# A gate matrix for 16384 experts: low parts of the weights on VectorE, one-hot rows of two keys in one operation

## The chip, the core and the metric

One core of a Trainium2 chip runs the whole program once. The metric is the time of one launch in device microseconds. Of the kernel before there are three timed runs, with a median of 3199.23 us (3198.02 to 3207.88).

The engines are called TensorE (PE in the profile, its weight loads PEld), VectorE (DVE), ScalarE (ACT), GpSimd (POOL) and SyncE (SP, which issues the DMAs here).

## What is computed

The reference is two transformer blocks, one after the other, on 512 tokens of width 1024, in 32-bit floats. The change touches one layer of the first block, a lookup among 16384 experts, cut to this:

```python
def peer(n, w_q, sub_keys, expert_u, expert_v):      # n: 512 tokens x 1024
    q = (nf @ w_q).reshape(t, PEER_HEADS, D_KEY)
    ...
    v1, i1 = lax.top_k(s1, TOPK)                     # 8 heads, 128 keys on either side
    v2, i2 = lax.top_k(s2, TOPK)
    cand = (v1[..., :, None] + v2[..., None, :]).reshape(t, PEER_HEADS, TOPK * TOPK)
    vals, ci = lax.top_k(cand, TOPK)
    ...
    idx = (e1 * N_KEYS + e2).reshape(t, PEER_HEADS * TOPK)
    gates = jax.nn.softmax(vals.astype(jnp.float32), axis=-1)
    ...
        ug = expert_u[ib]
        act = jax.nn.gelu(jnp.einsum("td,tkd->tk", xb, ug)) * gb
        vg = expert_v[ib]
        return jnp.einsum("tk,tkd->td", act, vg)
```

So each token has 128 chosen experts (8 heads times 16), named by a pair of keys (e1, e2) of 128 each, and a gate for each of them.

## The kernel before

The kernel does not gather experts. It treats all 16384 as a dense layer: hidden = gelu(expert_u x tokens), multiplied by a gate matrix that is zero where a token did not choose the expert, then expert_v x hidden. Hidden units are worked through in 128 rows of 128, one row for each value of the second key; the code calls such a row an expert row, and the texts here say "expert" for it. `up` (line 611) makes one: eight blocks of 128 input columns, each with three matmuls of 128x128 by 128x512 in `mm3` (lines 233 to 235). Three, because a 32-bit weight and a 32-bit input are each split into a high part, rounded to the matmul's format, and a low part, the remainder: high x high, high x low, low x high.

The weights come through `Stream` (line 77). A tile holds 16 blocks, so two experts. `fetch` asks SP for the 1 MB transfer into `raw` (three buffers). `block` calls `load_split` (line 210): for either half of 1024 columns ScalarE copies the high part into `wh` (line 216), then GpSimd subtracts it from the raw weight into `wl` (line 217). Both have two buffers (pool `sp`): one tile in use, one being made.

The layer has these steps. `route` makes queries, scores and the top 16 on VectorE (`top16`, line 799), and 37 experts run on TensorE beside it (`IN_ROUTE`). Then `build_g` (line 810) makes the gate matrix and the generator `fill`, which is `spills` over `up`, gives it the other 35 of the first 72 experts (`SPILL`). Their activations go to memory in groups of four (`act_d`). Then the main part goes over all 32 groups of experts: the gate is multiplied in (`gated`) and `down` adds the result to the tokens; the modulation vector of the second block (`ada`) is made beside it.

In `build_g` the partitions hold the 128 choices of a token. A pass of the loop handles `TB` = 8 tokens, so there are 64 passes. `hots` makes the one-hot rows with four VectorE operations of 128x1024 in 16 bits: `o1` (line 837) compares the first key with 0 to 127, `o2` (line 838) the second, and `og` (line 842), twice, multiplies `o2` by the high and by the low part of the gate. To keep runs of four adjacent values, keys and gates are first repeated four times (`repeated`, line 824; `DUP` = 4). TensorE multiplies `o1` by `og` (line 861), 16 matmuls a pass (two a token), ScalarE copies the sums from two PSUM buffers to `gs` (line 865), and every fourth pass SP writes 2 MB of it to `g_d` (line 869). `o1` has two buffers, `o2` one, `og` four, which is two passes of its two parts.

The order of the work: the program text gives priorities, and the framework lays out each engine's queue ahead of time from them, from the operands' dependences and from when buffers come free, so that an instruction can stand in its queue ahead of others that are earlier in the text. Only instructions named in `keep_in_program_order` are pinned. On the chip each queue is run strictly in order. One pass of the text is:

```python
            if t0 + TB < S:
                nxt = hots(t0 + TB)
            left = SPILL - IN_ROUTE
            if t0 // TB * left % (S // TB) < left:
                next(fill, None)
```

so one-hots are made a pass ahead, and an expert is run in 35 of the 64 passes, spread evenly: never do two passes in a row go without one.

Of the kernel before, what the change touches and what calls it, by code (L numbers as in the profile page):

```python
# [10 lines left out]
F32 = mybir.dt.float32  # L11
F32R = mybir.dt.float32r
BF16 = mybir.dt.bfloat16
F16 = mybir.dt.float16
# [8 lines left out]
P = 128  # L23
# [53 lines left out]
class Stream:  # L77
    def __init__(self, net, name, ub=UB, chunk=8, loads=1):
        self.net, self.ap, self.w, self.chunk, self.loads = net, net.A[name], ub * P, chunk * P, loads
        self.ub, self.raw, self.have = ub, {}, {}  # L80

    def fetch(self, b):
        if b not in self.raw and b not in self.have:
# [2 lines left out]
    def block(self, b):  # L86
        if b not in self.have:
            self.fetch(b)
            self.have = {k: v for k, v in self.have.items() if k >= b - 1}
            self.have[b] = self.net.load_split(self.raw.pop(b), self.w, self.chunk)  # L90
        return self.have[b]

    def unit(self, u, n=1):
# [31 lines left out]
def run(gen):  # L125
    for _ in gen:
        pass
# [12 lines left out]
class Net:  # L140
# [66 lines left out]
        if self.keeps:  # L207
            self.tc.keep_in_program_order(ins)

    def load_split(self, raw, w, chunk):  # L210
        nc = self.nc
        h = self.sp.tile([P, UB * P], F32R, tag="wh", name=self.nm("wh"))
        lo = self.sp.tile([P, UB * P], F32R, tag="wl", name=self.nm("wl"))
        for o in range(0, w, chunk):
            c = slice(o, min(o + chunk, w))
            self.keep(nc.scalar.copy(h[:, c], raw[:, c]))  # L216
            nc.gpsimd.tensor_tensor(lo[:, c], raw[:, c], h[:, c].bitcast(F32), ALU.subtract)  # L217
        return h, lo

    def split(self, src, tag=None, bufs=1, tags=None):  # L220
# [378 lines left out]
    def peer(self, X, pre=None):  # L599
        nc, tc = self.nc, self.tc  # L600
        act_d = self.dp.tile([SPILL // GE, P, GE, S], F32, tag="act_d", name="act_d")
        g_d = self.dp.tile([S // GB, P, E2, GB], F32, tag="g_d", name="g_d")
        v3 = lambda a: a.rearrange("p (b t) -> p b t", t=GB)
        with self.phase("pk"), ExitStack() as stack:
            ak = stack.enter_context(tc.tile_pool(name="ak", bufs=1, side="right"))
            a4_ = lambda: ak.tile([P, GE, S], F32, tag="a4", name=self.nm("a4"), bufs=2)
            pre = (pre or self.peer_norm(X)).ready()
            ns = pre.hs
            us, vs = Stream(self, "expert_u"), Stream(self, "expert_v")

            def up(gr, a4):
                for j in range(GE):
                    p = self.proj(us, (gr * GE + j) * KD, ns)
                    nc.scalar.activation(a4[:, j, :], p, AF.Gelu_apprx_tanh)
                    yield

            def spills():
                for gr in range(SPILL // GE):
                    a4 = a4_()
                    yield from up(gr, a4)  # L620
                    nc.sync.dma_start(act_d[gr], a4)

            def gated(a4, g4, As, pv):

                for j in range(GE):
                    a = a4[:, j, :]
                    nc.vector.tensor_tensor(v3(a), v3(a), g4[:, :, j, :], ALU.mult)  # L627
                    h, lo = (pv.tile([P, S], F32R, tag=t, name=self.nm(t), bufs=2 * GE) for t in ("ah", "al"))
                    nc.scalar.copy(h, a)  # L629
                    nc.vector.tensor_tensor(lo, a, h.bitcast(F32), ALU.subtract)  # L630
                    As.append((h, lo))
                    yield

            def down(at, As, beside):

                for n in range(KD):
                    p = self.ps()
                    for j in range(GE):
                        self.mm3(p, vs.unit((at * KD + n) * GE + j), As[j], j == 0, j == GE - 1)
                    nc.vector.tensor_tensor(X[n], X[n], p, ALU.add)  # L640
                    next(beside, None)
                run(beside)

            fill = spills()
            with tc.tile_pool(name="pr", bufs=1) as pr:
                e1T, e2T, gT = self.route(pre, pr, fill)
            with tc.tile_pool(name="pb", bufs=1) as pb:
                self.build_g(pb, e1T, e2T, gT, g_d, fill)
            run(fill)
            with tc.tile_pool(name="ad", bufs=1, side="right") as ad, tc.tile_pool(name="pv", bufs=1) as pv:  # L650
                def fetch(at):

                    if at == len(ORDER):
                        return None
                    gr, a4 = ORDER[at], a4_()
                    if gr * GE < SPILL:
                        nc.sync.dma_start(a4, act_d[gr])
                    g4 = ad.tile([P, S // GB, GE, GB], F32, tag="g4", name=self.nm("g4"), bufs=2)
                    nc.sync.dma_start(g4, g_d[:, :, gr * GE : (gr + 1) * GE, :].rearrange("b p e t -> p b e t"))
                    return a4, g4  # L660

                before = None
                mods = self.ada(ad)
                next(mods)
                nxt = fetch(0)
                for at, gr in enumerate(ORDER):
                    (a4, g4), As = nxt, []
                    if gr * GE >= SPILL:
                        for _ in up(gr, a4):
                            next(mods, None)  # L670
                    nxt = fetch(at + 1)
                    parts = gated(a4, g4, As, pv)
                    if gr * GE >= SPILL:
                        parts = chain(parts, (next(mods, None) for _ in range(KD - GE - 1)))
                    if before is None:
                        run(parts)
                    else:
                        down(*before, parts)
                    before = (at, As)
                run(mods)  # L680
                down(*before, iter(()))
# [117 lines left out]

    def top16(self, v, i, s, n):  # L800
        nc = self.nc
        tmp = self.small(n, tag="tk")
        nc.vector.max(v[:, 0:8], s)
        nc.vector.max_index(i[:, 0:8], v[:, 0:8], s)
        nc.vector.match_replace(tmp, v[:, 0:8], s, NEG)
        nc.vector.max(v[:, 8:16], tmp)
        nc.vector.max_index(i[:, 8:16], v[:, 8:16], tmp)

    def build_g(self, pb, e1T, e2T, gT, g_d, fill):
# [1 line left out]

        nc = self.nc
        io = pb.tile([P, P], F16, tag="io", name="io")
        ii = pb.tile([P, P], I32, tag="ioi", name="ioi")
        nc.gpsimd.iota(ii, [[1, P]], channel_multiplier=0)
        nc.vector.tensor_copy(io, ii)
        gh, gl = self.g(F16, "gh"), self.g(F16, "gl")
# [1 line left out]
        nc.vector.tensor_copy(gh, gT)  # L819
        nc.vector.tensor_tensor(gl, gT, gh, ALU.subtract)  # L820

        def repeated(src, tag):
            d = pb.tile([P, S, DUP], F16, tag=tag, name=tag)
            nc.vector.tensor_copy(d, src[:, :, None].to_broadcast([P, S, DUP]))
            return d

        k1, k2 = repeated(e1T, "k1"), repeated(e2T, "k2")
        parts = repeated(gh, "kh"), repeated(gl, "kl")
        four = [P, TB, P // DUP, DUP]
        v4 = lambda a: a.rearrange("p t (k d) -> p t k d", d=DUP)  # L830
        io4 = io.rearrange("p (k d) -> p k d", d=DUP)[:, None, :, :].to_broadcast(four)
        bc = lambda a, t0: a[:, t0 : t0 + TB, None, :].to_broadcast(four)

        def hots(t0):
            oh = lambda tag, bufs: pb.tile([P, TB, P], F16, tag=tag, name=self.nm(tag), bufs=bufs)
            o1, o2 = oh("o1", 2), oh("o2", 1)
            nc.vector.tensor_tensor(v4(o1), io4, bc(k1, t0), ALU.is_equal)
            nc.vector.tensor_tensor(v4(o2), io4, bc(k2, t0), ALU.is_equal)
            og = []
            for part in parts:  # L840
                og.append(oh("og", 4))
                nc.vector.tensor_tensor(v4(og[-1]), v4(o2), bc(part, t0), ALU.mult)
            return o1, og

        gs = None
        nxt = hots(0)
        for t0 in range(0, S, TB):
            o1, og = nxt
            if t0 + TB < S:
                nxt = hots(t0 + TB)  # L850
            left = SPILL - IN_ROUTE
# [4 lines left out]
            for q in range(TB // 4):  # L856
                p = self.ps("gg", 2)
                for i in range(4):
                    t = 4 * q + i
                    for j in range(2):  # L860
                        nc.tensor.matmul(
                            p[:, i * P : (i + 1) * P], o1[:, t, :], og[j][:, t, :], start=(j == 0), stop=(j == 1)
                        )
                r = t0 % GB + 4 * q
                nc.scalar.activation(
                    gs[:, :, r : r + 4], p.rearrange("p (t e) -> p e t", t=4), AF.Copy, scale=1.0 / GSCALE
                )
# [821 lines left out]
```

## Time and profile before

| | us |
|---|---|
| median of three runs | 3199.23 |
| the profiled execution | 3196.37 |
| its span in the trace | 3194.6 |
| TensorE busy in the span | 3048.8 |
| VectorE busy | 1905.5 |
| GpSimd busy | 1465.6 |
| ScalarE busy | 1049.6 |

The profiled execution's own time is 1.8 us more than its span. Busy time of TensorE is modelled, since matmuls are pipelined: a matmul's end in the trace lies behind the start of the next. Its rate is better read from the starts of neighbouring matmuls, or from how many there are in a stretch. A line number is the line of the kernel that issued an instruction; `xN` is how many there are in a row or group; a bracket gives the idle time of the engine just before, and what ended it.

### The profile page before, as it was taken

To read this page: it belongs to the slowest core of one execution; us is meant where nothing else is said; L and a number is where in the kernel's file an instruction comes from. 1 tells how busy PE (TensorE), PEld (TensorE's weight loads), DVE (VectorE), ACT (ScalarE), POOL (GpSimd) and SP (SyncE) were. 2 spreads that over 40 slices of the span, in tenths; PEclk is the share of its full clock that TensorE was granted. 3 is DMA by queue.
4 is the path that set the end of the run, shared out by engine and by line. 5 is a ranking of instruction groups with operands and counts; after the bars stand their busy time and mean duration, and the time that the engine had idled before them with its cause. 6 is when DMAs were issued, how large, how long until landed. Compare 5 with 4: busy or idle time off the path is not lost.

```text
span 3194.6 us, 38906 instructions
## 1 busy us (share of the span) xinstructions
PE 3048.8 (95%) x15428; PEld 2545.1 (80%) x15428; DVE 1905.5 (60%) x3262; ACT 1049.6 (33%) x1632; POOL 1465.6 (46%) x777
## 2 busy tenths in 40 slices
PE   8589999999999999999999988899999999999998
PEld 7478888777878888888888877778888887888887
DVE  8964778988667676676555566666211277552123
ACT  4232222444422322222222344343322234432222
POOL 5635666333345444454444443533444431234454
PEclk9889999999999999999999989999999999999999
DMA  3222333565775656665555311112222221122321
GB/s 135 73 79 93 119 119 139 198 237 208 264 247 197 211 199 207 214 224 193 202 188 177 109 67 60 53 41 79 89 91 105 99 76 38 53 92 76 116 88 65
DMA packets 131926, 424.88 MB, mean 133 GB/s; under 512 B 7824, under 2 KB 73872, under 8 KB 97184
## 3 DMA queue, kind: packets, MB, share of 16 engines
q1 hardware_dynamic: 131744, 422.40, 37.5%
q8 instruction: 121, 1.98, 0.3%
q14 instruction: 61, 0.50, 0.1%
HBM read 367.84 MB, written 54.53 MB: 132 GB/s over the span
## 4 chain that ended last, share of the span: by engine, by line
PE 47%; DVE 5%; issue 1%; ACT 1%; POOL 1%; DVEq 0%; POOLq 0%; ACTq 0%
PE mm L233 15%; PE mm L234 15%; PE mm L235 15%; DVE l L380 1%; PE sm L1239 1%; PE sm L1203 1%; DVE sq L297 0%; DVE m L371 0%; PE gg L1266 0%; PE sm L307 0%; PE gg L1260 0%; DVE x L980 0%; PE mm L1395 0%; PE sm L337 0%; POOL wl L217 0%
## 5 line engine op out<-in xcount | busy, mean ns | idle before, releaser
L217 POOL TENSOR_TENSOR wl<-raw,wh 128x1024 fp32r<-128x1024 f32 (+4 forms) x526 | 1280.2, 2456 | 1544.5 <-ACT wh L216 1537.2
L233 PE MATMUL mm<-h,wh 128*128 128x512 f32 (+1 forms) x2524 | 962.0, 382 | 24.3 <-DVE x L980 7.5
L235 PE MATMUL mm<-h,wl 128*128 128x512 f32 (+1 forms) x2524 | 951.6, 378 | 23.0 <-POOL wl L217 22.9
L234 PE MATMUL mm<-l,wh 128*128 128x512 f32 (+1 forms) x2428 | 924.9, 381 | 16.8 <-DVE l L228 12.4
L216 ACT CAST wh<-raw 128x1024 fp32r<-128x1024 f32 (+4 forms) x526 | 510.1, 996 | 938.1 <-issue 524.1
L235 PEld LDWEIGHTS mm<-h,wl 128*128 128x128 f32 x2524 | 482.0, 191 | 112.7 <-POOL wl L217 26.7
L233 PEld LDWEIGHTS mm<-h,wh 128*128 128x128 f32 x2524 | 482.5, 191 | 111.5 <-DVE x L980 8.7
L234 PEld LDWEIGHTS mm<-l,wh 128*128 128x128 f32 x2428 | 464.6, 191 | 100.6 <-DVE l L228 13.0
L233 PE MATMUL mm<-ah,wh 128*128 128x512 f32 x1024 | 399.3, 390 | 5.3 <-DVE x L640 5.3
L234 PE MATMUL mm<-al,wh 128*128 128x512 f32 x1024 | 399.1, 390 | 0.0
L235 PE MATMUL mm<-ah,wl 128*128 128x512 f32 x1024 | 399.0, 390 | 0.0
L942 DVE CUSTOM_DVE_ANT_0 aw<-aw,c 128x1024 f32<-128x1024 f32 x96 | 199.6, 2081 | 118.0 <-DMA aw<-in_ada_w 94.8
L640 DVE TENSOR_TENSOR x<-x,mm 128x512 f32<-128x512 f32 x256 | 172.6, 681 | 144.5 <-PE mm L235 144.5
L233 PEld LDWEIGHTS mm<-ah,wh 128*128 128x128 f32 x1024 | 192.6, 188 | 46.8 <-DVE x L640 4.4
L234 PEld LDWEIGHTS mm<-al,wh 128*128 128x128 f32 x1024 | 192.5, 188 | 40.1
L235 PEld LDWEIGHTS mm<-ah,wl 128*128 128x128 f32 x1024 | 192.6, 188 | 40.0
L1488 DVE TENSOR_TENSOR sg<-sg,mm 128x512 f32<-128x512 f32 (+1 forms) x48 | 30.9, 643 | 301.4 <-PE mm L235 288.0
L629 ACT CAST ah<-a 128x512 fp32r<-128x512 f32 x128 | 79.4, 621 | 333.8 <-DVE a L627 202.2
L980 DVE SCALAR_TENSOR_TENSOR x<-mm,mod,x 128x256 f32<-128x256 f32 (+1 forms) x112 | 66.5, 595 | 188.5 <-PE mm L235 188.4
L627 DVE TENSOR_TENSOR a<-a,g 128x512 f32<-128x512 f32 x128 | 139.8, 1118 | 61.6 <-DMA a<-act_d 47.4
L630 DVE TENSOR_TENSOR al<-a,ah 128x512 fp32r<-128x512 f32 x128 | 141.2, 1109 | 40.7 <-ACT ah L629 39.5
L233 PE MATMUL mm<-g,wh 128*128 128x512 f32 (+1 forms) x416 | 148.6, 357 | 0.0
(391 smaller groups left out, 3789.4 us busy)
## 6 DMA issues: line engine op xcount, KB each, us to landing
raw<-in_expert_u SPq DMA_DIRECT2D x64, 1024.0 KB, 5.3
raw<-in_expert_v SPq DMA_DIRECT2D x64, 1024.0 KB, 5.1
aw<-in_ada_w SPq DMA_DIRECT2D x96, 512.0 KB, 4.6
raw<-in_ffn_w_in SPq DMA_DIRECT2D x44, 1024.0 KB, 4.8
g_d<-gs SPq DMA_DIRECT2D x16, 2048.0 KB, 7.9
g<-g_d SPq DMA_DIRECT2D x32, 1024.0 KB, 6.3
act_d<-a SPq DMA_DIRECT2D x18, 1024.0 KB, 3.9
a<-act_d SPq DMA_DIRECT2D x18, 1024.0 KB, 4.8
```

What stands on the lines that cost most here:

```text
L216: self.keep(nc.scalar.copy(h[:, c], raw[:, c]))
L217: nc.gpsimd.tensor_tensor(lo[:, c], raw[:, c], h[:, c].bitcast(F32), ALU.subtract)
L233: nc.tensor.matmul(out, w[0], x[0], start=start, stop=False)
L234: nc.tensor.matmul(out, w[0], x[1], start=False, stop=False)
L235: nc.tensor.matmul(out, w[1], x[0], start=False, stop=stop)
L380: nc.vector.scalar_tensor_tensor(lo[:, c], t, sh(k), h[:, c].bitcast(F32), ALU.add, ALU.subtract)
L627: nc.vector.tensor_tensor(v3(a), v3(a), g4[:, :, j, :], ALU.mult)
L629: nc.scalar.copy(h, a)
L630: nc.vector.tensor_tensor(lo, a, h.bitcast(F32), ALU.subtract)
L640: nc.vector.tensor_tensor(X[n], X[n], p, ALU.add)
L942: nc.vector.tensor_tensor_reduce(w, w, c, 1.0, 0.0, ALU.mult, ALU.add, self.mod[:, i : i + 1])
L980: self.nc.vector.scalar_tensor_tensor(x, p, self.mod[:, o + n : o + n + 1], x, ALU.mult, ALU.add)
```

## The change

- `load_split` gets the engine of the subtraction as an argument, GpSimd as before, except for the tiles of `expert_u` that are asked for while `build_g` runs: there it is VectorE.
- In that time `up` asks for the tile of the next expert right behind an expert's activation. For the first expert of a tile this is the same tile, for the second the next one.
- The two keys lie side by side in one tensor, as do the gate's two parts, so that one VectorE operation of 128x2048 makes the one-hots of both keys (`oh`, in place of `o1` and `o2`). The two multiplications stay two, and write the two halves of one `og`. Both tiles have two buffers.
- The scratch of `top16` has two buffers in place of four, and the index tile `ii` comes from the common pool of 512-column tiles.

```diff
     def __init__(self, net, name, ub=UB, chunk=8, loads=1):
...
+        self.eng = net.nc.gpsimd
...
-            self.have[b] = self.net.load_split(self.raw.pop(b), self.w, self.chunk)
+            self.have[b] = self.net.load_split(self.raw.pop(b), self.w, self.chunk, self.eng)
...
-    def load_split(self, raw, w, chunk):
+    def load_split(self, raw, w, chunk, eng):
...
-            nc.gpsimd.tensor_tensor(lo[:, c], raw[:, c], h[:, c].bitcast(F32), ALU.subtract)
+            eng.tensor_tensor(lo[:, c], raw[:, c], h[:, c].bitcast(F32), ALU.subtract)
...
                     nc.scalar.activation(a4[:, j, :], p, AF.Gelu_apprx_tanh)
+                    if us.eng is nc.vector:
+                        us.block((gr * GE + j + 1) * KD // UB)
                     yield
...
+                us.eng = nc.vector
                 self.build_g(pb, e1T, e2T, gT, g_d, fill)
+            us.eng = nc.gpsimd
             run(fill)
...
-        tmp = self.small(n, tag="tk")
+        tmp = self.small(n, tag="tk", bufs=2)
...
-        ii = pb.tile([P, P], I32, tag="ioi", name="ioi")
+        ii = self.g(I32, "ioi")[:, :P]
...
-        def repeated(src, tag):
-            d = pb.tile([P, S, DUP], F16, tag=tag, name=tag)
-            nc.vector.tensor_copy(d, src[:, :, None].to_broadcast([P, S, DUP]))
+        def repeated(two, tag):
+
+            d = pb.tile([P, S, 2, DUP], F16, tag=tag, name=tag)
+            for i, src in enumerate(two):
+                nc.vector.tensor_copy(d[:, :, i, :], src[:, :, None].to_broadcast([P, S, DUP]))
             return d
 
-        k1, k2 = repeated(e1T, "k1"), repeated(e2T, "k2")
-        parts = repeated(gh, "kh"), repeated(gl, "kl")
-        four = [P, TB, P // DUP, DUP]
-        v4 = lambda a: a.rearrange("p t (k d) -> p t k d", d=DUP)
+        keys, gates = repeated((e1T, e2T), "kk"), repeated((gh, gl), "kg")
+        four = [P, 2 * TB, P // DUP, DUP]
+        v4 = lambda a: a.rearrange("p t i (k d) -> p (t i) k d", d=DUP)
         io4 = io.rearrange("p (k d) -> p k d", d=DUP)[:, None, :, :].to_broadcast(four)
-        bc = lambda a, t0: a[:, t0 : t0 + TB, None, :].to_broadcast(four)
+        bc = lambda a, t0: a[:, t0 : t0 + TB].rearrange("p t i d -> p (t i) d")[:, :, None, :].to_broadcast(four)
 
         def hots(t0):
-            oh = lambda tag, bufs: pb.tile([P, TB, P], F16, tag=tag, name=self.nm(tag), bufs=bufs)
-            o1, o2 = oh("o1", 2), oh("o2", 1)
-            nc.vector.tensor_tensor(v4(o1), io4, bc(k1, t0), ALU.is_equal)
-            nc.vector.tensor_tensor(v4(o2), io4, bc(k2, t0), ALU.is_equal)
-            og = []
-            for part in parts:
-                og.append(oh("og", 4))
-                nc.vector.tensor_tensor(v4(og[-1]), v4(o2), bc(part, t0), ALU.mult)
-            return o1, og
+            oh, og = (pb.tile([P, TB, 2, P], F16, tag=t, name=self.nm(t), bufs=2) for t in ("oh", "og"))
+            nc.vector.tensor_tensor(v4(oh), io4, bc(keys, t0), ALU.is_equal)
+            for i in range(2):
+                nc.vector.tensor_tensor(
+                    og[:, :, i, :].rearrange("p t (k d) -> p t k d", d=DUP),
+                    oh[:, :, 1, :].rearrange("p t (k d) -> p t k d", d=DUP),
+                    gates[:, t0 : t0 + TB, i, None, :].to_broadcast([P, TB, P // DUP, DUP]), ALU.mult,
+                )
+            return oh, og
...
-                            p[:, i * P : (i + 1) * P], o1[:, t, :], og[j][:, t, :], start=(j == 0), stop=(j == 1)
+                            p[:, i * P : (i + 1) * P], oh[:, t, 0, :], og[:, t, j, :], start=(j == 0), stop=(j == 1)
```

## Rows read from the trace of the kernel before

**Rows 1.** Windows: start:end, length, then busy us (count) of each engine, clock, DMA.
```profile
core 0: us, PE busy (x) PEld busy (x) DVE busy (x) ACT busy (x) POOL busy (x), PEclk, DMA share, GB/s
...
559.00:829.00 270.00, 257.72 (x1844) 207.69 (x1843) 236.86 (x256) 117.39 (x199) 99.30 (x35) 0.99 0.56 215
...
829.00:860.00 31.00, 31.00 (x139) 25.64 (x138) 12.38 (x14) 13.06 (x17) 13.55 (x6) 1.00 0.90 300
...
1000.00:1100.00 100.00, 100.00 (x443) 82.81 (x442) 72.22 (x69) 30.09 (x40) 51.68 (x20) 1.00 0.56 196
```
**Rows 2.** Timeline of PE, two places: start us, us, engine, line, operation [idle before, releaser].
```profile
609.53 1.07 PE L861 MATMUL gg<-og,o 128*128 128x128 f16 x16
610.40 0.47 PE L233 MATMUL mm<-h,wh 128*128 128x512 f32 x1
610.72 0.39 PE L234 MATMUL mm<-l,wh 128*128 128x512 f32 x1
...
664.28 0.47 PE L233 MATMUL mm<-h,wh 128*128 128x512 f32 x1
665.08 0.23 PE L861 MATMUL gg<-og,o 128*128 128x128 f16 x1 [0.33 <-DVE og L842]
665.68 1.00 PE L861 MATMUL gg<-og,o 128*128 128x128 f16 x15 [0.37 <-DVE og L842]
```
**Rows 3.** Waits in 559 to 829 us: total, times, longest.
```profile
PE gg L861 <- DVE og L842: 11.5, 25, 2.9
```
**Rows 4.** Groups by line in 559 to 829 us: busy us, mean ns, idle before.
```profile
L217 POOL TENSOR_TENSOR wl<-raw,wh 128x1024 fp32r<-128x1024 f32 x35 | 100.4, 2888 | 177.3 <-ACT wh L216 177.3
L837 DVE TENSOR_TENSOR o<-io,k 128x1024 f16<-128x1024 f16 x64 | 78.9, 1232 | 1.6 <-PE gg L861 1.6
L842 DVE TENSOR_TENSOR og<-o,kl 128x1024 f16<-128x1024 f16 x64 | 76.6, 1197 | 0.0
...
L838 DVE TENSOR_TENSOR o<-io,k 128x1024 f16<-128x1024 f16 x64 | 48.4, 756 | 1.7
L842 DVE TENSOR_TENSOR og<-o,kh 128x1024 f16<-128x1024 f16 x64 | 46.2, 721 | 23.9 <-PE gg L861 21.7
```
**Rows 5.** Timelines of POOL and of DVE around one tile's subtractions.
```profile
610.66 5.65 POOL L217 TENSOR_TENSOR wl<-raw,wh 128x1024 fp32r<-128x1024 f32 x2 [8.44 <-ACT wh L216]
...
611.19 2.88 DVE L837 TENSOR_TENSOR o<-io,k 128x1024 f16<-128x1024 f16 x1
613.99 2.87 DVE L842 TENSOR_TENSOR og<-o,kl 128x1024 f16<-128x1024 f16 x1
616.90 0.69 DVE L838 TENSOR_TENSOR o<-io,k 128x1024 f16<-128x1024 f16 x1
617.51 0.68 DVE L837 TENSOR_TENSOR o<-io,k 128x1024 f16<-128x1024 f16 x1
```
**Rows 6.** Timeline of PE at the loop's second pass.
```profile
564.07 0.39 PE L234 MATMUL mm<-l,wh 128*128 128x512 f32 x1
567.33 0.23 PE L861 MATMUL gg<-og,o 128*128 128x128 f16 x1 [2.87 <-DVE og L842]
```
**Rows 7.** Single lines of DVE: duration ns minimum/median/maximum, first and last start.
```profile
L630 DVE TENSOR_TENSOR al<-a,ah x128: 676/693/2877, 857.4 to 1794.6; 128x512 fp32r<-128x512 f32 x128
...
L942 DVE CUSTOM_DVE_ANT_0 aw<-aw,c x96: 1209/1713/3466, 846.1 to 1419.4; 128x1024 f32<-128x1024 f32 x96
...
L824 DVE COPY k<-T x2: 1217/1218/1218, 553.2 to 554.6; 128x2048 f16<-128x2048 f16 x2
```
**Rows 8.** Timeline of ACT around the copies of high parts.
```profile
609.54 1.05 ACT L216 CAST wh<-raw 128x1024 fp32r<-128x1024 f32 x1 [4.69 <-issue]
...
610.98 1.08 ACT L865 ACTIVATE gs<-gg 128x512 f32<-128x512 f32 x2
611.94 1.06 ACT L216 CAST wh<-raw 128x1024 fp32r<-128x1024 f32 x1
...
625.60 1.05 ACT L216 CAST wh<-raw 128x1024 fp32r<-128x1024 f32 x1 [4.47 <-issue]
```

More of the change, by code (lines that the diff above doesn't have):

```diff
@@ L847, in build_g @@
         for t0 in range(0, S, TB):
-            o1, og = nxt
+            oh, og = nxt
             if t0 + TB < S:
```

## The prediction

> **What bounds the kernel now.** The edit lives in one stretch, the loop that builds the gate matrix, so I read the windows first, to see which engine fills it. From 559 to 829 us, 270 us, TensorE is busy 257.7 us, VectorE 236.9, GpSimd 99.3, ScalarE 117.4, at a granted clock of 0.99 [rows 1]. In the 31 us behind it TensorE is busy all the time, and in a plain stretch later it runs 443 matmuls in 100 us without a pause [rows 1]. So time saved in the loop should reach the end, and only idle TensorE time in the loop can be saved.
>
> How much is that? Busy time of TensorE is modelled, so I count work by spacing. A 512-column matmul costs 100 / 443 = 0.2257 us [rows 1]. One expert in the loop is 8 x 3 = 24 of them, and 35 experts run there (72 - 37, by the constants): 35 x 24 x 0.2257 = 189.6 us. One pass of the loop adds 16 gate matmuls. They start at 609.53, the next expert matmul at 610.40, and the one behind that at 610.72 instead of 610.63: 610.72 - 609.53 - 0.2257 = 0.96 us for a pass [rows 2], 64 passes 61.7 us. Together 251.3 of 270 us. **At most 18.7 us is to be had**, 0.6% of the run.
>
> Who takes it? The list of waits puts 11.5 us, 25 times, on gate matmuls that wait for VectorE's gated one-hots (`og`, L842), and lists none of TensorE's for the low parts [rows 3]. The next views say why VectorE is late, though it has only four short operations a pass. Grouped by line, its four operations have the same shape, but mean 1232 and 1197 ns for two of them and 756 and 721 for the others [rows 4]. The timeline separates these: a free one takes 0.69 us; those that meet a GpSimd subtraction take 2.88 and 2.87 us, just as long as the two subtractions beside them (5.65 us) [rows 5]. One instruction is held behind each subtraction. A held one costs 2.88 - 0.69 = 2.2 us, a tile with its two subtractions 4.4 us. VectorE's share of 88% is therefore mostly waiting inside instructions: 256 operations at a spacing of 0.6 us (616.90 to 617.51, [rows 5]) are 154 us of work, not 237.
>
> The price on TensorE: at 664.28 an expert matmul starts, the next gate matmul only at 665.08, and the one after that at 665.68 [rows 2]. Against 0.2257 and 0.054 us (16 in 0.87 us, [rows 2]) that is 0.57 + 0.55 = 1.12 us. Such a pair comes ten times between 618 and 820 us. The idle column shows 0.33 and 0.37 for it, as it counts from modelled ends. Ten pairs are 7.0 of the 11.5 us, 2.87 is one long wait at 567.33 [rows 6], and the other four make up 1.6, which with the same 0.2 on each is about 2.5 by spacing. So by spacing: pairs 11.2, four early waits 2.5, the long one 3.0 (564.07 + 0.2257 to 567.33 [rows 6]): 16.7 of the 18.7 us. The other 2 us lie in small gaps, which I leave as they are.
>
> **The change part by part.** *Low parts on VectorE.* 36 subtractions of 128x1024 leave GpSimd (35 of them in the stretch [rows 4]); nothing else of GpSimd's is there, so no instruction of VectorE is held any more: -35 x 2.2 = -77 us of VectorE. They come back on VectorE. No row shows this subtraction there. Bounds: from below, twice the free 128x512 subtraction of the same types, less one start (0.676 minimum, [rows 7]), about 1.2 us; from above, the 128x1024 two-input operation on VectorE at its median of 1.71 us, which has held ones in it, with a minimum of 1.209 [rows 7]. I take 1.21, or 1.13 between starts, as GpSimd is silent: 36 x 1.13 = +41 us. The copy to the high part stays on ScalarE, in the same number.
>
> *A tile ahead.* The new call asks for the next tile at the end of the second expert of a tile instead of the start of the next one, a few instructions earlier in program order. The queues already run further ahead than that: ScalarE's copy starts at 609.54, just as a tile's last matmul frees its buffer, and the tile it fills is first used when the tile in use is done, where the next such copy starts, at 625.60 [rows 8]. I cost this at nothing. What covers the low parts is that whole tile, 16 us; without it TensorE would wait the 4.4 us that copies and subtractions take.
>
> *New wait in VectorE's queue.* A subtraction waits for its copy. The first copy ends at 610.6, the second only starts at 611.94, behind evictions, and ends at 613.0 [rows 8]. Whatever one-hots stand behind it wait too, and gate matmuls wait for those. If both subtractions go in front of a pass's one-hots, VectorE loses 2.3 us of work and up to 1.3 of waiting a tile, against 4.4 now; if one-hots go between, nothing waits.
>
> *One-hots.* Two operations of 1024 become one of 2048 columns; the nearest row is the 128x2048 copy of the same type, 1.218 us [rows 7], against two at 0.6 + 0.08 between starts: -0.07 x 64 = -4.5 us. It may lose something too: one buffer now holds both keys, so the second key's one-hot, which was free early, also waits for TensorE's pass two earlier. A pass needs 1.13 + 0.6 + 0.6 = 2.35 us of VectorE, and between the end of one pass and the start of the one two later there is always an expert (5.4 us) and a pass: covered. Without the expert it would lack 1.4 us.
>
> *Copies ahead of the loop* keep their count and size, with a gap of four in the output. Bounds: as now, or 4 x 1.1 us more if the gap halved their rate; I take nothing. The index tile takes a slot of the g pool, and the top-16 scratch has two buffers for four; both are used by VectorE in its own order, and a slot late by some 0.5 us hides behind 10 us of VectorE preparation. Queue of SP: same transfers, raw tiles are freed up to 3 us sooner.
>
> *Sum.* VectorE in the loop: 64 x 2.35 + 41 = 191 us, 76% of the 251 that TensorE needs. The ten pairs go (11.2) and the four early waits (2.5). Of the long first wait I take half (1.5): GpSimd's two subtractions hold the one-hots there now, and in their place VectorE does the same tile's two, 2.3 us, at the same spot. The small gaps stay. 15.2 us. The profiled execution took 3196.37 us (span 3194.6); 3181.2 for it, and 2.9 us more for the median of 3199.23: **3184 us**.
>
> **The rivals.** *VectorE as late as before.* The subtractions stand ahead of one-hots and wait there for ScalarE's copies: 2.3 + 1.3 + 1.05 for the first copy = 4.6 us a tile, which equals the 4.4 of the held ones. For it: the order of [rows 8], and a queue that cannot pass a waiting instruction. Against: one-hots are ready before the second copy. Pairs stay half or whole: 0 to 8 us saved, about 3195.
>
> *VectorE is full, and gets more.* Read by busy time, 236.9 + 41 - 4.5 = 273 us against a stretch of 270: 3 us slower, with its waits up to 10, 3203 to 3210. Against it, the 81 us of held time of [rows 5]. The Trainium skill (Perfetto Trace Analysis, Optimizing Scalar/DVE Operations) advises moving work from a saturated VectorE to other engines, GpSimd among them, the reverse of this edit, though it adds that the two share a read port; the rows show that second point.
>
> *Slower: one-hots lose their rate.* The new views step over the other key. If a 16-bit operation then ran at the pace of the 32-bit one (1.13 us for 1024), a pass would cost 2.2 + 2 x 1.13 = 4.5 us, 64 of them and the subtractions 329 us: 59 slower, 3258. It decides from a pass of (270 - 41) / 64 = 3.6 us. Against: the innermost four stay adjacent, as in the views now, which run 1024 in 0.6 us [rows 5]. The Trainium skill (VectorE: DVE Perf Modes, What auto-detection actually checks) asks for 16-bit tensors with step one, which would keep the rate.
>
> *It does not do what it says.* The flag is read when a tile is asked for, inside the loop, so it does; but the queues are ordered anew by the framework, in the routing too: a few us either way.
>
> **How the numbers follow.** A measurement tells 0.3% from no change, 9.6 us. Forecast 0.60 (10 to 19 us saved). As late as before 0.25, nearly all within 0.3%. VectorE full 0.05, between same and slower. Lost rate 0.05, slower. Order disturbed 0.05, split between same and slower. That is faster 0.60, same 0.29, slower 0.11. Low end: all 18.7 us, 2.7 more if the clock's 0.99 became 1.00 (1% of 270), and 2 for the spread of runs, 3176. High end: no gain, and 1 us of spread, 3200. Above it lies about 0.12, below it little.
>
> **What would show it.** Right: GpSimd idle in the loop; no operation of L842 over 0.7 us; subtraction near 1.2 us; the one-hot near 1.2; TensorE's waits for `og` from 25 to a few; loop of about 255 us; the granted clock 0.99 to 1.00. Wrong: VectorE idle for ScalarE's copies with `og` waits of the old size; one-hots of 2.2 us; TensorE waiting for low parts; or a loop that is shorter with the time lost again behind 829 us.

## The result, and the profile after

| | before | after |
|---|---|---|
| median, us | 3200.23 (6 runs, 3198.02 to 3207.88) | 3178.80 (6 runs, 3172.54 to 3183.84) |
| ratio, 95% interval | | 0.9938 (0.9927 to 0.9950) |
| profiled execution's span, us | 3194.6 | 3175.4 |

The changed kernel is 0.6% faster: 21.4 us by the medians, 16 to 23 by the interval. Forecast was 3184 in a range of 3176 to 3200, which is 16 us less than the kernel before takes here: the right side and mechanism, too small by about a quarter of the 21.4. The median lies in the range.

Line numbers of the matmuls are one higher now (L234 to L236), the one-hots are L842, the products L844, the subtractions L218. The loop ends, with SP's last write of `g_d`, at 811.0 in place of 829.1 us. Its windows, in the columns of [rows 1]:

```profile
core 0: us, PE busy (x) PEld busy (x) DVE busy (x) ACT busy (x) POOL busy (x), PEclk, DMA share, GB/s
559.00:810.00 251.00, 250.95 (x1831) 204.80 (x1830) 192.15 (x225) 114.61 (x194) 0.39 (x1) 1.00 0.60 231
810.00:841.00 31.00, 31.00 (x138) 25.65 (x137) 11.79 (x13) 13.98 (x19) 14.71 (x6) 1.00 0.89 295
```

Beside [rows 1]: the loop takes 251 us for 270, TensorE is busy in all of it by its modelled ends, GpSimd in none but the last 0.4 us, and VectorE, which does more than before, is busy 192 us where it was 237. What became of the held instructions of [rows 4] stands in the single lines (duration in ns, minimum/median/maximum), one of a product before and three after:

```profile
L842 DVE TENSOR_TENSOR og<-o,kl x64: 679/684/2878, 561.1 to 822.4; 128x1024 f16<-128x1024 f16 x64
...
L842 DVE TENSOR_TENSOR oh<-io,kk x64: 1211/1219/1227, 557.7 to 802.0; 128x2048 f16<-128x2048 f16 x64
L844 DVE TENSOR_TENSOR og<-oh,kg x128: 680/684/693, 560.0 to 803.9; 128x1024 f16<-128x1024 f16 x128
...
L218 DVE TENSOR_TENSOR wl<-raw,wh x36: 1208/1218/1227, 547.5 to 800.2; 128x1024 fp32r<-128x1024 f32 x36
```

No instruction of the loop is held any longer: the longest product takes 0.693 us, where the maximum was 2.88. The waits of the loop after, 559 to 810 us, to set beside [rows 3]:

```profile
...
ACT wh L217 <- PE mm L235: 72.4, 16, 4.6
ACT a L615 <- PE mm L236: 53.6, 16, 3.4
DVE wl L218 <- ACT wh L217: 43.3, 15, 3.8
PEld L867 <- issue: 13.6, 51, 0.3
ACT gs L871 <- PE gg L867: 10.2, 13, 3.5
DVE oh L842 <- PE gg L867: 9.2, 15, 0.6
...
```

TensorE's 25 waits for `og` are gone. The new wait that the first rival was made of is there, 43.3 us of VectorE's queue standing for ScalarE's copies, and TensorE pays nothing for it. The timeline of VectorE for one tile shows why:

```profile
616.86 1.23 DVE L218 TENSOR_TENSOR wl<-raw,wh 128x1024 fp32r<-128x1024 f32 x1 [2.51 <-ACT wh L217]
618.01 2.35 DVE L842 TENSOR_TENSOR oh<-io,kk 128x2048 f16<-128x2048 f16 x2
620.28 2.49 DVE L844 TENSOR_TENSOR og<-oh,kg 128x1024 f16<-128x1024 f16 x4
622.68 1.22 DVE L218 TENSOR_TENSOR wl<-raw,wh 128x1024 fp32r<-128x1024 f32 x1
624.51 1.23 DVE L842 TENSOR_TENSOR oh<-io,kk 128x2048 f16<-128x2048 f16 x1 [0.61 <-PE gg L867]
```

The second subtraction stands behind two passes of one-hots, not in front of them, so only the first waits, at a time when VectorE has run out of other work: both one-hot buffers are full until TensorE's pass that began at 615.8 us frees one. Which order the framework would lay out was not worked out beforehand; it came out well.

**Two places outside the steps.** One lies ahead of the loop. There GpSimd made three low parts in a row at the routing's tail, and VectorE's short instructions on the way to the transposes were held too. Timelines of GpSimd and VectorE before:

```profile
540.77 7.46 POOL L217 TENSOR_TENSOR wl<-raw,wh 128x1024 fp32r<-128x1024 f32 x3
...
543.65 2.36 DVE L781 TENSOR_SCALAR e<-cd 128x512 int32<-128x512 int32 x1
545.93 2.85 DVE L777 TENSOR_TENSOR vals<-vals,gr 128x512 f32<-128x512 f32 x1
```

and after, where the tile that is asked for first in the loop has its low parts made here already, on VectorE:

```profile
545.58 0.35 DVE L786 TENSOR_SCALAR e<-cd 128x512 int32<-128x512 int32 x1
545.86 0.67 DVE L782 TENSOR_TENSOR vals<-vals,gr 128x512 f32<-128x512 f32 x1
...
547.46 2.34 DVE L218 TENSOR_TENSOR wl<-raw,wh 128x1024 fp32r<-128x1024 f32 x2
```

TensorE waited 2.5 us for this chain before (`PE sm L794 <- DVE e1f L785`), 0.2 after.

The other is TensorE's clock. Windows around its two long idle times, before:

```profile
548.00:552.00 4.00, 2.50 (x15) 2.19 (x16) 3.07 (x6) 0.00 (x0) 0.23 (x1) 0.86 0.98 383
552.00:555.00 3.00, 3.00 (x10) 2.37 (x9) 2.90 (x6) 0.00 (x0) 0.23 (x1) 0.62 0.60 254
564.00:568.00 4.00, 1.13 (x6) 0.45 (x5) 3.97 (x4) 0.79 (x3) 2.72 (x1) 0.99 0.14 18
568.00:574.00 6.00, 6.00 (x42) 4.75 (x41) 5.13 (x9) 2.31 (x5) 0.00 (x0) 0.72 0.42 165
```

and after:

```profile
552.00:555.00 3.00, 3.00 (x15) 2.47 (x14) 3.00 (x5) 0.00 (x0) 0.00 (x0) 1.00 1.00 423
564.00:568.00 4.00, 4.00 (x31) 3.06 (x30) 4.00 (x5) 1.59 (x4) 0.00 (x0) 1.00 0.02 4
568.00:574.00 6.00, 6.00 (x50) 4.47 (x49) 5.85 (x9) 3.60 (x7) 0.00 (x0) 1.00 0.79 302
```

TensorE stood still from 547.0 to 549.5 and from 564.5 to 567.3 us. Behind either, the granted clock was the lower of its two levels (1.2 of 2.4 GHz) for part of the time, 0.62 and 0.72 in the mean; after, without the two idle times, it is 1.00 throughout. By these rows the lower clock took 0.14 x 4 + 0.38 x 3 = 1.7 us ahead of the loop and 0.28 x 6 = 1.7 us in it. Such an idle time is not always followed by it. In the first experiment below TensorE stood as long at nearly the same place (2.46 of the 4 us), and the clock stayed at 1.00:

```profile
548.00:552.00 4.00, 1.54 (x11) 1.13 (x10) 3.58 (x6) 0.60 (x1) 1.55 (x2) 1.00 1.00 334
552.00:555.00 3.00, 3.00 (x16) 2.48 (x16) 2.85 (x7) 0.00 (x0) 0.06 (x1) 1.00 0.91 382
```

### The profile page after: what moved, and what is told of

The parts are those of the page before. It is cut to its first block, busy times and chain, and to the rows that moved or that the text cites. A ratio compares the mean times of both kernels' runs of the same rounds, so it can differ in the third digit from the quotient of the medians.

```text
span 3175.4 us, 38844 instructions
## 1 busy us (share of the span) xinstructions
PE 3046.8 (96%) x15428; PEld 2543.4 (80%) x15428; DVE 1862.6 (59%) x3234; ACT 1049.2 (33%) x1632; POOL 1358.5 (43%) x741
## 4 chain that ended last, share of the span: by engine, by line
PE 48%; DVE 5%; issue 1%; ACT 1%; POOL 0%; DVEq 0%; POOLq 0%; ACTq 0%
PE mm L234 15%; PE mm L235 15%; PE mm L236 15%; DVE l L381 1%; PE sm L1245 1%; PE sm L1209 1%; DVE sq L298 0%; DVE m L372 0%; PE gg L1272 0%; PE sm L308 0%; PE gg L1266 0%; DVE x L986 0%; PE mm L1401 0%; POOL wl L218 0%; PE sm L338 0%
## 5 line engine op out<-in xcount | busy, mean ns | idle before, releaser
L218 POOL TENSOR_TENSOR wl<-raw,wh 128x1024 fp32r<-128x1024 f32 (+1 forms) x490 | 1172.6, 2415 | 1634.1 <-ACT wh L217 1366.4
L234 PE MATMUL mm<-h,wh 128*128 128x512 f32 (+1 forms) x2524 | 963.4, 382 | 26.3 <-DVE x L986 7.4
L236 PE MATMUL mm<-h,wl 128*128 128x512 f32 (+1 forms) x2524 | 953.7, 379 | 23.7 <-POOL wl L218 23.5
L235 PE MATMUL mm<-l,wh 128*128 128x512 f32 (+1 forms) x2428 | 926.8, 382 | 16.5 <-DVE l L229 12.1
L236 PEld LDWEIGHTS mm<-h,wl 128*128 128x128 f32 x2524 | 483.0, 192 | 115.0 <-POOL wl L218 27.9
L234 PEld LDWEIGHTS mm<-h,wh 128*128 128x128 f32 x2524 | 483.5, 192 | 114.0 <-DVE x L986 8.7
L234 PE MATMUL mm<-ah,wh 128*128 128x512 f32 x1024 | 399.3, 390 | 4.3 <-DVE x L643 4.3
L236 PE MATMUL mm<-ah,wl 128*128 128x512 f32 x1024 | 399.0, 390 | 0.0
L234 PEld LDWEIGHTS mm<-ah,wh 128*128 128x128 f32 x1024 | 192.6, 188 | 45.7 <-DVE x L643 3.4
L236 PEld LDWEIGHTS mm<-ah,wl 128*128 128x128 f32 x1024 | 192.6, 188 | 40.3
L234 PE MATMUL mm<-g,wh 128*128 128x512 f32 (+1 forms) x416 | 148.6, 357 | 0.0
```

The source lines that it names most:

```text
L218: eng.tensor_tensor(lo[:, c], raw[:, c], h[:, c].bitcast(F32), ALU.subtract)
L234: nc.tensor.matmul(out, w[0], x[0], start=start, stop=False)
L235: nc.tensor.matmul(out, w[0], x[1], start=False, stop=False)
L236: nc.tensor.matmul(out, w[1], x[0], start=False, stop=stop)
```

## The experiments

Each was timed against the kernel before on the same chip (4 to 12 runs of each); where the diff starts from the changed kernel, it says so.

**One-hots alone.** From the changed kernel:

```diff
-                us.eng = nc.vector
```

> The changed kernel with the low parts left on GpSimd throughout (the call ahead never fires then), so the one-hot layout and the buffers alone. Theory A (held VectorE operations are the cause): GpSimd's subtractions are back in the loop, 35 of them, and hold one VectorE operation each, up to 2.9 us; the loop takes about 267 us (251 of TensorE work and the waits), the ratio to the kernel before is 0.997 to 1.002, as the layout saves 4.5 us of VectorE alone. Theory B (the gain comes from fewer and larger VectorE operations or from the buffers): ratio about 0.994, the loop near 252 us.

3201.10 us, ratio 1.0010 (1.0001 to 1.0018). VectorE's products are held again, up to 2.88 us, and TensorE waits for them as before. Grouped lines and the one wait of TensorE, 557 to 830 us and 560 to 805 us, of this run:

```profile
L843 DVE TENSOR_TENSOR og<-oh,kg 128x1024 f16<-128x1024 f16 x128 | 153.0, 1237 | 2.1
L218 POOL TENSOR_TENSOR wl<-raw,wh 128x1024 fp32r<-128x1024 f32 x34 | 110.8, 3279 | 161.8 <-ACT wh L217 161.8
...
PE gg L866 <- DVE og L843: 12.4, 19, 3.9
```

The layout alone gains nothing.

**The engine alone.** From the kernel before, with the engine passed to `load_split` as in the change:

```diff
-            nc.gpsimd.tensor_tensor(lo[:, c], raw[:, c], h[:, c].bitcast(F32), ALU.subtract)
+            eng.tensor_tensor(lo[:, c], raw[:, c], h[:, c].bitcast(F32), ALU.subtract)
...
+                us.eng = nc.vector
                 self.build_g(pb, e1T, e2T, gT, g_d, fill)
+            us.eng = nc.gpsimd
```

> The kernel before with one edit: the low parts of the tiles asked for in the loop on VectorE, with four one-hot operations a pass and without the call ahead. Theory A: no VectorE operation of the loop over 1.3 us, VectorE busy about 196 us in it, ratio 0.992 to 0.996. Theory B: ratio near 1.000.

3175.48 us, ratio 0.9927 (0.9913 to 0.9941): the whole gain, with four one-hot operations a pass. Theory B falls with these two runs. One point of the expectation failed. Without the call ahead the loop's last tile is asked for when the flag is back at GpSimd, so VectorE makes 34 low parts and GpSimd two, and beside these two, and only there, operations of VectorE are held:

```profile
792.13 5.63 POOL L218 TENSOR_TENSOR wl<-raw,wh 128x1024 fp32r<-128x1024 f32 x2 [243.07 <-PE gg L864]
...
792.63 2.88 DVE L840 TENSOR_TENSOR o<-io,k 128x1024 f16<-128x1024 f16 x1
795.43 2.87 DVE L845 TENSOR_TENSOR og<-o,kl 128x1024 f16<-128x1024 f16 x1
```

**Without the call ahead.** From the changed kernel:

```diff
-                    if us.eng is nc.vector:
-                        us.block((gr * GE + j + 1) * KD // UB)
```

> The changed kernel without the call that asks for the next tile behind the activation. Prediction's step: the queues already run a tile ahead, so the call is worth nothing, ratio 0.992 to 0.996, TensorE never waits for a low part. Rival: the low parts come later on a VectorE that has the one-hots to do first, TensorE waits for them, up to 4 us a tile and 18 tiles: ratio up to 1.01.

3178.97 us, ratio 0.9938 (0.9925 to 0.9950), as with the call. No wait of TensorE for a low part stands in the loop. Costing it at nothing was right within what can be measured. It does have an effect: without it GpSimd makes the last tile here too (793.65 us, 6.23 us), and TensorE waits 1.1 us for `og` again.

**GpSimd put back beside.** From the changed kernel:

```diff
             eng.tensor_tensor(lo[:, c], raw[:, c], h[:, c].bitcast(F32), ALU.subtract)
+            if eng is nc.vector:
+                nc.gpsimd.tensor_tensor(raw[:, c], raw[:, c], h[:, c].bitcast(F32), ALU.subtract)
```

> The changed kernel, and behind each subtraction of VectorE in the loop a GpSimd subtraction of the same size and operands that overwrites the raw tile, which nothing reads after that. Theory A: VectorE operations are held again, 36 times 1.7 to 2.2 us, and do the low parts too: 191 + 60 to 80 = 250 to 270 us of VectorE in the loop, which is as much as TensorE needs or more; the gain is lost, ratio 0.997 to 1.006. Rival (GpSimd beside VectorE costs nothing, the order of the queues made the gain): ratio 0.994, as without it.

3196.16 us, ratio 0.9995 (0.9987 to 1.0004). The gain is lost to an operation whose result nobody reads. Grouped lines, 557 to 830 us:

```profile
L846 DVE TENSOR_TENSOR og<-oh,kg 128x1024 f16<-128x1024 f16 x127 | 118.0, 979 | 0.9
L220 POOL TENSOR_TENSOR raw<-raw,wh 128x1024 f32<-128x1024 f32 x34 | 114.5, 3366 | 159.5 <-DVE wl L218 154.8 <-PE gg L869 4.7
L844 DVE TENSOR_TENSOR oh<-io,kk 128x2048 f16<-128x2048 f16 x62 | 109.1, 1783 | 1.0 <-PE gg L869 1.0
L218 DVE TENSOR_TENSOR wl<-raw,wh 128x1024 fp32r<-128x1024 f32 x34 | 41.3, 1215 | 3.2 <-ACT wh L217 3.2
```

The one-hot operation that takes 1219 ns alone has a mean of 1783 beside GpSimd, and GpSimd's own operation one of 3366, where the shortest of them takes 2392: each is held by the other. The added operation keeps buffers in use as well, and ScalarE's copies wait for it (23.5 us). That is not what costs the gain: all of TensorE's waits in the loop are for `og` (15.2 us, 30 times), none for a low part.

**Twice on VectorE.** As the last, but with `eng` in place of `nc.gpsimd` in the added line, so 36 more subtractions of VectorE.

> The changed kernel with each subtraction of VectorE in the loop followed by a second one of the same size on VectorE (it overwrites the raw tile, which nothing reads after). VectorE in the loop 192 + 41 = 233 us of 251. Theory A with its cover (a tile's lead and 24% of free VectorE time): nearly all hidden, ratio to the kernel before 0.993 to 0.996. Rival: the low parts are only just covered, each further microsecond in VectorE's queue delays the one-hots: 0.997 to 1.003.

3181.04 us, ratio 0.9947 (0.9935 to 0.9960). In 560 to 805 us VectorE is busy 223.2 of 245 us (191.2 in the changed kernel), and TensorE still has no wait of the loop in the list. The cover is wide: what spoiled the loop was not VectorE's work but its being held.

**From the routing on.** From the changed kernel, the flag set ahead of `route`, where TensorE has no idle time to give back.

> The changed kernel with VectorE also for the low parts of the tiles that are asked for in the routing ahead of the loop, some 18 tiles more. GpSimd holds VectorE operations there too, but TensorE does not wait for them (99% busy and more from 300 to 540 us). Theory A with its condition (only idle TensorE time counts): no further gain, ratio 0.993 to 0.996. Rival 1 (held VectorE time is worth time anywhere): 18 x 4.4 us less, up to 0.980. Rival 2 (VectorE, 72 to 90% busy there, gets 41 us more and becomes the bound): above 0.997.

3221.22 us, ratio 1.0076 (1.0064 to 1.0089), 1.4% slower than the changed kernel. That is rival 2's side, but not for its reason: from 300 to 540 us VectorE is busy 157 of 240 us, less than before (181). Waits in that stretch:

```profile
POOL C L739 <- DVE V L808: 129.3, 6, 22.8
...
PE mm L236 <- POOL wl L218: 31.7, 6, 5.4
```

TensorE waits 31.7 us for low parts of another weight, the queries', which stay on GpSimd. They stand in its queue behind the pair sums (L739) and the products of the same round (L757), and the pair sums wait for VectorE's top 16. In one round the pair sums could start only at 408.64 us, and GpSimd came to the low part at 424.27:

```profile
408.64 2.15 POOL L739 TENSOR_TENSOR C<-V 128x32 f32<-128x32 f32 x6 [21.30 <-DVE V L808]
...
422.76 1.55 POOL L757 TENSOR_TENSOR w<-eq,E 128x800 f32<-128x800 bf16 x1 [0.51 <-DVE eq L755]
424.27 4.69 POOL L218 TENSOR_TENSOR wl<-raw,wh 128x1024 fp32r<-128x1024 f32 x2
...
426.68 0.80 PE L236 MATMUL mm<-h,wl 128*128 128x512 f32 x1 [5.36 <-POOL wl L218]
```

ScalarE's two copies for this tile had started at 419.02 and 420.46 and taken 1.04 us each, so a free GpSimd could have begun about 4 us earlier. The clock does its part: 0.92 in the stretch, 0.99 before.

**Smaller pieces on GpSimd.** From the kernel before:

```diff
-            us, vs = Stream(self, "expert_u"), Stream(self, "expert_v")
+            us, vs = Stream(self, "expert_u", chunk=4), Stream(self, "expert_v")
```

> The kernel before with the tiles of the first expert weight copied and subtracted in quarters of 512 columns in place of halves of 1024, the subtractions still on GpSimd: 70 in the loop of some 1.3 to 1.5 us. If an operation of VectorE is held as long as the one GpSimd operation beside it runs, the longest takes 1.5 us in place of 2.9, and a tile costs 4 x 0.7 = 2.8 us of held time in place of 4.4: ratio 0.995 to 0.999. If what counts is GpSimd's busy time in total, no change: 0.999 to 1.002.

3186.66 us, ratio 0.9964 (0.9951 to 0.9977). The number is the first theory's, the held time is not. Single lines of the products, and the grouped subtraction in 560 to 820 us:

```profile
L842 DVE TENSOR_TENSOR og<-o,kl x64: 679/684/1787, 556.7 to 815.1; 128x1024 f16<-128x1024 f16 x64
...
L217 POOL TENSOR_TENSOR wl<-raw,wh 128x512 fp32r<-128x512 f32 x68 | 106.8, 1590 | 156.0 <-ACT wh L216 156.0
```

A held operation is as long as the shorter GpSimd piece allows, 1.79 in place of 2.88 us, but about four a tile are held instead of two: at most 4 x (1.78 - 0.69) = 4.4 us, which is what two held ones cost before. TensorE's waits in the loop fall only to 7.9 us, 16 times, from 11.5 and 25. Of the 9.7 us between the two profiled executions 3.6 are there at the end of the routing's top 16 (520.7 for 524.4 us); the next runs look at that stretch.

**The engine, and smaller pieces.** The engine alone with the edit of the last.

> The kernel before with the low parts of the loop on VectorE (as in the run with the engine alone), and copies and subtractions of this weight in quarters of 512 columns. What is left of TensorE's gaps in the loop are some 27 of 0.17 to 0.25 us, 5.7 us together, in front of gate matmuls while ScalarE has a 1.05 us copy between its evictions. If that copy is their cause, shorter ones take half of them: ratio 0.991 to 0.993 where the engine alone gave 0.9927. Rival (other cause, or more instructions cost as much): 0.9925 to 0.995.

3169.65 us, ratio 0.9910 (0.9896 to 0.9925). In the expected range, but the reason given falls: gate matmuls still start some 0.2 us late two dozen times in the loop, counted from their starts, as often as with the engine alone. What the pieces add lies in the routing. Waits of TensorE from 250 to 500 us and a window there, in the changed kernel:

```profile
345.00:380.00 35.00, 34.65 (x161) 28.60 (x160) 26.00 (x106) 9.23 (x12) 23.41 (x24) 1.00 0.33 120
...
PE mm L236 <- POOL wl L218: 4.7, 6, 3.0
```

and here:

```profile
345.00:380.00 35.00, 35.00 (x165) 29.23 (x164) 26.45 (x109) 10.11 (x18) 24.46 (x29) 1.00 0.34 120
...
PE mm L236 <- POOL wl L218: 1.9, 1, 1.9
```

There the low part on GpSimd is just late, 0.33 us every 35 us and 3.0 once, as in the kernel before:

```profile
373.73 0.50 PE L235 MATMUL mm<-h,wl 128*128 128x512 f32 x1 [0.33 <-POOL wl L217]
```

The matmul needs the first columns alone, and a shorter first piece is ready sooner.

**Three on one chip:** the change with the smaller pieces, the change, the engine alone.

> The changed kernel with copies and subtractions of the first expert weight in quarters. If the gain of quarters lies in the routing (GpSimd's shorter pieces let the matmul that needs a low part start sooner) it adds to this kernel as to the one with the engine alone: ratio 0.990 to 0.992, some 6 to 8 us less at 540 us, the same loop. If it came from the loop's evictions: no lead at 540 us, a shorter loop. If it was the spread of runs: 0.993 to 0.995.

> The changed kernel again, beside the other two on one chip: ratio 0.9925 to 0.995.

> The kernel with the engine alone again, on the same chip as the changed one. If the one-hot layout is worth what it saves VectorE (4.5 us), this one is 1 to 4 us slower than the changed kernel; if VectorE's time in the loop is covered, the same within 2 us; if the layout costs something (one buffer for both keys), 2 to 5 us faster.

3170.92 us, 0.9923 (0.9910 to 0.9937); 3179.03 us, 0.9944 (0.9930 to 0.9957); 3175.78 us, 0.9940 (0.9925 to 0.9954). The last top 16 of the routing's first kind starts at 521.8 us in the first and at 526.0 in the second, both having started at 272; so some 4 us of the smaller pieces arise in the routing, fewer than the 6 to 8 expected. The loop is as long in both: the lead at its last eviction is 4.6 us (805.5 and 810.1). The other 3 us of the two profiled executions arise behind the loop. With the engine alone the smaller pieces gain nothing there (from the last eviction to the end 2366.0 us, 2364.7 without them), so that these 3 us are not shown to be theirs.

Between the second and the third no difference can be told (3.3 us by the medians, with intervals that overlap), so the layout is worth nothing measurable here. The lowest median is that of the engine with smaller pieces and without the layout, 3169.65 us. It is faster than both kernels, but not told apart from the change with smaller pieces, which ran on another chip.

## Why the prediction was right, and where its size was off

- *What bounds.* Right: only idle TensorE time could be saved, and what was saved stayed saved: 18.1 us earlier at the loop's end, 19.2 at the end of the span. That 251.3 us of work were worked out and the loop now takes 251 is partly luck. The sum took 35 whole experts, 840 matmuls of 512 columns; the windows hold 820 before (1844 - 1024, [rows 1]) and 807 after (1831 - 1024), as some of the experts' work lies outside. At the same prices that is 246.8 us of work in 270, and 243.8 in 251: TensorE was late or slow for 23 us, not 18.7, and still is for 7.
- *Held instructions as the cause.* Right, shown by four runs: with GpSimd's work gone, VectorE's operations are short, but for two beside the one tile that GpSimd kept (engine alone); with that work there, they are long (one-hots alone); put back, it takes the gain away; doubled VectorE work does not. The Trainium skill (SBUF — State Buffer, SBUF: two separate sides) says that VectorE, with two inputs from SBUF or in a mode that uses both ports, and GpSimd lock a port pair in turn, and that the other blocks for the whole instruction. The traces agree in both directions: 2.88 for 0.69 us on VectorE, a mean of 3.37 for 2.39 on GpSimd.
- *Prices.* The subtraction was taken at 1.21 and is 1.218; the merged one-hot at 1.22 and is 1.219; VectorE in the loop at 191 and is 192.
- *The rivals.* Fullness by busy time fell most clearly: an engine at 88% took on 44 us of work and dropped to 77%. The advice named there (the Trainium skill, Perfetto Trace Analysis, Optimizing Scalar/DVE Operations), to unload a saturated VectorE on other engines, GpSimd among them, leaves the subtraction where the kernel before has it, at 3200 us; its own remark that the two share a port fits the traces. The one-hots kept their rate.
- *The mis-sized terms.* 15.2 us were summed, from the profiled execution, all of it for the loop. From the end of the routing's top 16 (524.4 before, 526.3 after) to the loop's end the two traces differ by 18.1 + 1.9 = 20.0 us.
  - *In the loop* the sum was nearly right. From the first to the last gate matmul it took 265.1 us (562.3 to 827.4) and takes 248.6 (560.7 to 809.4): 16.4 less. "Of the long first wait I take half (1.5)": all 3.0 us went, +1.5; the two subtractions of that tile were done while VectorE had time. The clock's 0.99 was read as a mean over the loop, worth 2.7 us at the range's edge; in the loop it was one fall behind one idle time, +1.7. Against that, a pair was taken at 1.12 us and is 1.03: 0.2257 us were taken off for the expert matmul inside the pair, but one that stands right behind gate matmuls takes 0.32 to the next start (610.40 to 610.72, [rows 2]). That is -0.9 for ten pairs. And the small gaps grew, from 16 of 0.22 us to 28 of 0.14 to 0.17 by the starts, -1.0. That makes 16.5.
  - *Ahead of the loop* nothing was summed, and the rest came from there. "A slot late by some 0.5 us hides behind 10 us of VectorE preparation" looked at this stretch for losses alone and missed that its instructions were held as well: TensorE's wait of 2.5 us fell to 0.2, and the fall of the clock behind it, 1.7 us, went too. Together 4.0; the traces show 3.5 to the first gate matmul, with two more expert matmuls done by then.
- The small gaps that "stay" did stay in kind. Their cause is open: shorter copies on ScalarE did not remove them.

## What to carry to other kernels

An engine's busy share can be made of instructions that are held: compare minimum and maximum of one shape in the single lines before calling an engine full, and find what runs beside the long ones. Moving work onto the engine that looks full can then free it. But the same move pays only where the bound engine waits, and only if no third engine's queue stands behind the work that grows: in the routing it cost 1.4%.

## What was not expected of the hardware

- GpSimd and VectorE hold one another in turn. Cutting GpSimd's operations into halves shortens each hold (2.88 to 1.79 us) and raises their number, so that the held time of a tile hardly changes.
- An instruction of VectorE with one tensor input was held as well: the shift of integers at L781 took 2.36 us beside GpSimd and 0.35 without it.
- Idle times of TensorE of 2.5 and 2.9 us each cost 1.7 us more behind them, at the lower clock; another of 2.5 us cost nothing more.
- Equal kernels differ by some us from run to run (the changed kernel's runs lie between 3172.5 and 3183.8 us), as much as many edits are worth, and part of it arises ahead of the routing: with the engine alone the top 16 started at 269.8 us in one execution and at 266.7 in another. Stretches between two marks are compared more safely than whole times.
